# 256-column matmuls take 64 columns of each half in turn, and pages and U tiles move to other places modulo 512 bytes

## The chip, the cores and the metric

The kernel runs on one core of one Trainium2 chip. The metric is the device time of one execution in microseconds. A core has five engines that matter here: TensorE (PE in the profile; its weight loads have a row of their own, PEld), VectorE (DVE), ScalarE (ACT), GpSimd (POOL) and SyncE (SP, which issues most of the transfers). Before the change the median of three runs was 759.83 us (757.2 to 761.03).

## The reference, cut to what matters

One layer of a gated short convolution between two norms, for 1024 positions of 1024 channels, with an inner width of 2048. Everything is float32.

```python
u = rms_norm(x, pre_norm)                                  # 1024 x 1024
z, bg, cg, v = jnp.split(u @ w_in, 4, axis=-1)             # w_in 1024 x 8192
y = bg * causal_dwconv(cg * v, conv_w) * jax.nn.silu(z)    # 3 taps, 1024 x 2048
h = x + rms_norm(y @ w_out, post_norm)                     # w_out 2048 x 1024
```

So there are two large matrix products, `u @ w_in` and `y @ w_out`, and elementwise work between them.

## The kernel before, in words

**Seven products in place of eight.** Both large products are cut into blocks of two by two, and of each the kernel computes seven block products, named a to g, whose operands are sums and differences of blocks. Products a, c, d and e of `u @ w_in` always run at full block size, with 512 columns per matmul. Products b, f and g are, for most channel groups, cut a second time in the same way: seven smaller products a' to g' with 256 columns per matmul (`deep_product`, line 1463). The output product does the same: `out_mm` (line 1890) has 512 columns, and its products b and f are made of seven small ones (`small_mm`, line 1983, called by `product_b` and `product_f`).

**Three matmuls for one.** Each operand is split into a high and a low part of a reduced float32 type, and a product is the sum low*high + high*low + high*high. So each 128-row step of a product is three matmuls, each with its own weight load of 128 x 128.

**The two reads of TensorE.** In a matmul call the third argument is the moving operand (128 partitions, 256 or 512 columns of 4 bytes), the second the weights (128 partitions, 128 columns, 512 bytes in a row per partition). While one matmul streams, the weights of the next are loaded. The moving operand and the output are both rearranged by `walk` (line 865), which sets the order in which the columns are taken: `"p (h c n) -> p c h n"` with c=4 and n=4 takes 4 columns (16 bytes), jumps 64 bytes on, takes 4, and so on to the end of the row, then starts again 16 bytes further; four passes make the whole. It is the same for 256 and 512 columns.

**Where things lie.** Per partition there are seven slots of 16 KB for U tiles (`Shelves`, line 219: u_a to u_g, and later the operands of the output product, ou, oy, oA, oB, ox) and 32 pages of 2 KB (`Pages`, line 235), which hold raw weights, sums, split weights (w.., dw..) and snapshots. A pool named tmp (line 1345) holds the convolution's rows and the moving operands of the second level (`ubc` to `ugg`, tag "ub", 2 KB each, line 1412). `U_LAYOUT` (line 205) says which slots form which of two groups and how many unused bytes follow each group; `gap` (line 213) reserves them. In the built program, modulo 512 bytes: pages at 64; the slots that first hold u_b, u_f and u_g at 64; those of u_a, u_c, u_d and u_e at 384; the "ub" tiles at 448. All steps inside these tiles that a matmul addresses are multiples of 512 bytes, so a tile's place modulo 512 is that of every operand in it.

**What sets the order.** From the second channel group on, all instructions are recorded first and put in order by a planner (`Plan.arrange`), with costs and corrections in the table PLAN; every recorded call is then issued from line 292, so nearly all rows of the profile name that line, and one goes by tile names. The change does not touch the planner or its table.

**Counts.** Over 16 channel groups, b is cut again for 14, f for 13 and g for 12 (`LAST`, line 820): 39 times 7 products of 6 matmuls, 1638 matmuls of 256 columns, of which 24 of each 42 stream from a U tile (a', b', e', f') and 18 from "ub" tiles (c', d', g'). `product_b` and `product_f` add 168 each: 1974 in all, of 4320 matmuls.

Of the kernel before, what the change touches and what calls it, by code (L numbers as in the profile page):

```python
# [89 lines left out]
class View:  # L90
# [3 lines left out]
    def __init__(self, tile, steps, ids, dtype):  # L94
        self.tile, self.steps, self.ids, self.dtype = tile, steps, ids, dtype
# [104 lines left out]
class Op:  # L200
# [2 lines left out]


U_LAYOUT = (
    ((0, 3, 4), 320),
    ((1, 2, 5, 6), 192),
)
LOW_PAGES = (3, 10, 11, 13, 15, 16, 5, 6, 8, 9)
U_SLOTS = (5, 4, 2, 6, 1, 3, 0, 0, 5, 2, 6, 4, 1, 3, 0, 5, 2, 6, 4, 1, 6, 3, 0, 4, 2, 5, 6, 1, 0, 3, 2, 4, 5, 6, 0, 4, 1, 5, 3, 6, 0, 2)  # L210
# [2 lines left out]
def gap(ctx, tc, name, size):  # L213

    if size:
        ctx.enter_context(tc.tile_pool(name=name, bufs=1)).tile([128, size // 4], F32, tag=name, name=name)


class Shelves:

    def __init__(self, ctx, tc):
        self.at, self.slots = {}, list(U_SLOTS)
        for n, (slots, room) in enumerate(U_LAYOUT):
            pool = ctx.enter_context(tc.tile_pool(name=f"up{n}", bufs=1))
            self.at.update({s: pool for s in slots})
            if n == 0:
                self.low = ctx.enter_context(tc.tile_pool(name="low_pages", bufs=1))
            gap(ctx, tc, f"room{n}", room)

# [439 lines left out]
def kernel(  # L669
# [23 lines left out]
    HB = 512  # L693
# [169 lines left out]
    banks = {}  # L863

    def walk(a):
        return a.rearrange("p (h c n) -> p c h n", c=4, n=4)

    def product(p, i, ks=None):

        w = wt[p, i]  # L870
        which = {"b": "y", "e": "v", "f": "v"}.get(i, "x")
        first = i in "abe"
        if first and (p, which) not in banks:
            banks[p, which] = bank(f"p{which}_{p}")
        ps = banks[p, which]
        for k in range(KH) if ks is None else ks:
            hi, lo = (h[:, k * P : (k + 1) * P] for h in w)
            last = k == KH - 1
            nc.tensor.matmul(walk(ps), lo, walk(UH[i][:, k]), start=first and k == 0, stop=False, skip_group_check=True)
            nc.tensor.matmul(walk(ps), hi, walk(UL[i][:, k]), start=False, stop=False, skip_group_check=True)  # L880
            nc.tensor.matmul(walk(ps), hi, walk(UH[i][:, k]), start=False, stop=last, skip_group_check=True)
# [157 lines left out]

    mixed = ExitStack()  # L1040
    head = ExitStack()
    gap(ctx, tc, "room_tmp", 352)
    hp = plan.pool(head.enter_context(tc.tile_pool(name="head", bufs=1, reuse_waits="tile")), 1)

    xa = hp.tile([P, TH, D], F32, tag="xa", name="xa")
# [634 lines left out]
    for p in range(2, len(PAIRS)):  # L1680
        q, c = p + 1, p // 2
# [91 lines left out]
    for n, slot in enumerate(slots):  # L1773
        if slot[2:]:
            z, i, c = slot
# [24 lines left out]
        i, p = slot  # L1800
# [324 lines left out]
```

## Time and profile before

| | before |
|---|---|
| median of 3 runs | 759.83 us |
| the profiled execution, its own time | 758.6 us |
| its span, first to last instruction | 756.8 us |
| mean granted TensorE clock | 0.999 |
| PE busy | 744.9 us (98%), 4320 matmuls |
| PEld busy | 658.8 us (87%), 4320 loads |
| DVE busy | 677.8 us (90%) |
| ACT busy | 458.7 us (61%) |
| POOL busy | 462.4 us (61%) |

A matmul's length in the profile (some 275 ns for 256 columns, some 385 ns for 512) is longer than the distance between two of them, since they are pipelined and their ends are modelled. What a matmul costs is therefore read from the starts: the start of one run of matmuls minus the start of the run before, divided by the count. Starts are given to 0.01 us.

### The profile page before, as it was taken

The page shows a single profiled execution, that of the slowest core. Times are in us where ns is not written, and L with a number is a line of the kernel's source. Part 1 is how long each engine was busy: PE and PEld are TensorE (multiplying, and loading weights), DVE is VectorE, ACT ScalarE, POOL GpSimd, SP SyncE. Part 2 cuts the span into 40 slices and gives each one's busy share as a digit, 9 for nine tenths or more (in the row PEclk, how much of TensorE's full clock was granted, in tenths as well). Part 3 has the DMA queues.
Part 4 walks back from the last instruction along what each step waited for, and adds up shares of the span by engine and source line. Part 5 has one row for each costly group of instructions (what it writes and reads, how often), then busy time and mean ns, then how long its engine had stood idle before and what let it go on. Part 6 is the DMA issues. An engine that isn't in the chain of part 4 may idle for free.

```text
span 756.8 us, 12810 instructions
## 1 busy us (share of the span) xinstructions
PE 744.9 (98%) x4320; PEld 658.8 (87%) x4320; DVE 677.8 (90%) x1022; ACT 458.7 (61%) x880; POOL 462.4 (61%) x416
## 2 busy tenths in 40 slices
PE   8999999999999999999999999999999999999996
PEld 6888889898989899989998998999888889889885
DVE  6899998999998988989989999898999999877994
ACT  7765588675656565656556565656553656565831
POOL 2509997889685778696788677695739100600421
PEclk9999999999999999999999999999999999999999
DMA  9213325253333547576859393928465998666842
GB/s 318 74 49 91 111 75 160 103 145 125 107 119 98 174 112 209 132 192 164 258 125 269 81 256 73 272 98 223 118 179 178 343 369 307 195 227 204 281 152 111
DMA packets 117137, 130.11 MB, mean 172 GB/s; under 512 B 7320, under 2 KB 74704, under 8 KB 116944
## 3 DMA queue, kind: packets, MB, share of 16 engines
q1 hardware_dynamic: 112560, 120.77, 50.0%
q0 software_dynamic: 4352, 8.39, 7.3%
q8 instruction: 34, 0.56, 0.3%
q14 instruction: 31, 0.25, 0.1%
q10 hardware_dynamic: 160, 0.14, 0.1%
HBM read 101.74 MB, written 44.30 MB: 193 GB/s over the span
## 4 chain that ended last, share of the span: by engine, by line
PE 83%; DVE 6%; POOL 3%; issue 3%; DMA 3%; ACT 2%; SPq 0%; DVEq 0%; POOLq 0%; ACTq 0%
PE px L292 34%; PE pv L292 13%; PE po_x L292 8%; PE px2b L292 4%; PE px2f L292 3%; PE pp L292 3%; PE po_v L292 3%; PE px2g L292 3%; PE pv2b L292 2%; PE pv2f L292 2%; PE pb_x L292 1%; PE py L292 1%; PE py2b L292 1%; DMA raw<-in_sc_w_in 1%; PE pv2g L292 1%
## 5 line engine op out<-in xcount | busy, mean ns | idle before, releaser
L292 PE MATMUL px<-u_a,wah 128*128 128x512 f32 x248 | 75.8, 386 | 0.0
L292 PE MATMUL px<-u_d,wdh 128*128 128x512 f32 x248 | 75.5, 385 | 0.0
L292 PE MATMUL px<-u_c,wch 128*128 128x512 f32 x248 | 74.8, 382 | 0.0
L292 PE MATMUL pv<-u_e,weh 128*128 128x512 f32 x248 | 74.7, 381 | 0.0
L292 ACT COPY beside<-raw 128x512 f32<-128x512 f32 x67 | 39.6, 591 | 34.2 <-DVE wal L292 9.9
L292 PEld LDWEIGHTS px<-u_a,wah 128*128 128x128 f32 x248 | 46.5, 187 | 8.6
L292 PEld LDWEIGHTS px<-u_d,wdh 128*128 128x128 f32 x248 | 46.5, 187 | 8.6
L292 DVE SCALAR_TENSOR_TENSOR cv<-gpad,cw,cv 128x1024 f32<-128x1024 f32 x32 | 51.0, 1593 | 3.0 <-ACT cv L292 2.8
L292 PEld LDWEIGHTS px<-u_c,wch 128*128 128x128 f32 x248 | 46.5, 188 | 7.8
L292 PEld LDWEIGHTS pv<-u_e,weh 128*128 128x128 f32 x248 | 46.5, 188 | 7.6
L292 POOL TENSOR_TENSOR sf<-raw,sc 128x512 f32<-128x512 f32 x30 | 47.1, 1569 | 5.7 <-DVE sc L292 3.9
L292 PE MATMUL px<-u_d,wdl 128*128 128x512 f32 x124 | 48.1, 388 | 0.0
L292 PE MATMUL px<-u_a,wal 128*128 128x512 f32 x124 | 48.0, 387 | 0.0
L292 PE MATMUL px<-u_c,wcl 128*128 128x512 f32 x124 | 47.7, 384 | 0.2 <-DVE wcl L292 0.2
L292 PE MATMUL pv<-u_e,wel 128*128 128x512 f32 x124 | 47.4, 382 | 0.0
L292 POOL TENSOR_TENSOR sc<-se,raw 128x512 f32<-128x512 f32 x25 | 35.9, 1437 | 18.3 <-DVE se L292 9.4
L292 POOL TENSOR_TENSOR rs_post<-ve_post,minus_half 128x1 f32<-128x1 f32 x7 | 6.5, 941 | 65.9 <-DVE ve_post L292 65.9
L292 POOL TENSOR_TENSOR raw<-raw,raw 128x512 f32<-128x512 f32 x31 | 43.1, 1389 | 4.2 <-DVE se L292 3.8
L292 POOL TENSOR_TENSOR se<-raw,raw 128x512 f32<-128x512 f32 x22 | 31.3, 1423 | 18.1 <-DMA raw<-in_sc_w_in 13.9
L292 ACT COPY sna<-px 128x512 f32<-128x512 f32 x30 | 17.6, 585 | 35.9 <-PE px L292 32.1
L292 DVE TENSOR_TENSOR wcl<-sc,wch 128x512 fp32r<-128x512 f32 x31 | 31.9, 1028 | 5.1 <-ACT wch L292 5.1
L292 POOL TENSOR_TENSOR sne<-snc,sne 128x512 f32<-128x512 f32 x12 | 18.3, 1529 | 21.6 <-ACT snc L292 21.6
(486 smaller groups left out, 2624.5 us busy)
## 6 DMA issues: line engine op xcount, KB each, us to landing
raw<-in_sc_w_in SPq DMA_DIRECT2D x128, 256.0 KB, 5.1
y_d<-cv SPq DMA_DIRECT2D x16, 512.0 KB, 2.7
s_d<-s SPq DMA_DIRECT2D x32, 256.0 KB, 4.8
t_d<-in_sc_w_out POOLq DMA_DIRECT2D x16, 512.0 KB, 8.3
tb<-in_sc_w_out SPq DMA_DIRECT2D x16, 256.0 KB, 3.6
t_d<-in_sc_w_out SPq DMA_DIRECT2D x16, 256.0 KB, 4.8
t_d<-t_d SPq DMA_DIRECT2D x16, 256.0 KB, 4.6
s<-y_d SPq DMA_DIRECT2D x16, 256.0 KB, 4.8
```

The source lines that it names most:

```text
L292: getattr(engine, name)(*(self.plain(a) for a in args), **{k: self.plain(a) for k, a in kw.items()})
```

## The change: the column order of short matmuls, and four addresses

`walk` now tells two cases apart. For 512 columns nothing changes. For 256 columns it takes columns 0 to 63, 128 to 191, 64 to 127 and 192 to 255: runs of 64 columns (256 bytes), and between the two runs of a pair a jump to the same place of the other half, 512 bytes on. The output is walked in the same order, so the same values go to the same places.

The unused bytes are dealt out differently: a new reserve of 64 bytes ahead of the low pages, 64 and 448 bytes after the two groups of slots, and 160 in place of 352 ahead of tmp. In the built program, modulo 512 bytes, pages are then at 128, u_b, u_f and u_g (and what later lies in their slots) still at 64, u_a, u_c, u_d and u_e at 192, and the "ub" tiles at 320. Taken as the moving operand's place minus that of the weights, modulo 512:

| moving operand, weights | before | after |
|---|---|---|
| u_a, u_c, u_d, u_e; a page | 320 | 64 |
| u_b, u_f, u_g; a page | 0 | 448 (64 short of 512) |
| "ub" tiles; a page | 384 | 192 |
| output product, both in slots | 0, 192 or 320 | 0, 128 or 384 |

```diff
 U_LAYOUT = (
-    ((0, 3, 4), 320),
-    ((1, 2, 5, 6), 192),
+    ((0, 3, 4), 64),
+    ((1, 2, 5, 6), 448),
 )
...
             pool = ctx.enter_context(tc.tile_pool(name=f"up{n}", bufs=1))
             self.at.update({s: pool for s in slots})
             if n == 0:
+                gap(ctx, tc, "room_low", 64)
                 self.low = ctx.enter_context(tc.tile_pool(name="low_pages", bufs=1))
             gap(ctx, tc, f"room{n}", room)
...
     def walk(a):
-        return a.rearrange("p (h c n) -> p c h n", c=4, n=4)
+        if a.shape[-1] == HB:
+            return a.rearrange("p (h c n) -> p c h n", c=4, n=4)
+        return a.rearrange("p (h c n) -> p c h n", h=2, n=64)
...
-    gap(ctx, tc, "room_tmp", 352)
+    gap(ctx, tc, "room_tmp", 160)
```

No instruction is added, removed or moved to another place on any engine; what differs is the form of the 256-column matmuls. On PE, at the first such place of the recorded part, where product a (tile px, operand u_a, 512 columns) is followed by second-level products (px2b from a "ub" tile, pv2b from u_b), before the change:

```order
L292 MATMUL px_1176<-u_a,wal_1108 128x4x32x4
L292 MATMUL px_1176<-u_a,wah_1071 128x4x32x4 x2
L292 MATMUL px2b_1101<-ubch_deep,dwb1l_1160 128x4x16x4
L292 MATMUL px2b_1101<-ubcl_deep,dwb1h_1104 128x4x16x4
L292 MATMUL px2b_1101<-ubch_deep,dwb1h_1104 128x4x16x4
L292 MATMUL pv2b_1219<-u_b,dwb1l_1160 128x4x16x4
L292 MATMUL pv2b_1219<-u_b,dwb1h_1104 128x4x16x4 x2
```

The same rows of PE after the change (the numbers in names count tiles, and all rise by four):

```order
L293 MATMUL px_1180<-u_a,wal_1112 128x4x32x4
L293 MATMUL px_1180<-u_a,wah_1075 128x4x32x4 x2
L293 MATMUL px2b_1105<-ubch_deep,dwb1l_1164 128x2x2x64
L293 MATMUL px2b_1105<-ubcl_deep,dwb1h_1108 128x2x2x64
L293 MATMUL px2b_1105<-ubch_deep,dwb1h_1108 128x2x2x64
L293 MATMUL pv2b_1223<-u_b,dwb1l_1164 128x2x2x64
L293 MATMUL pv2b_1223<-u_b,dwb1h_1108 128x2x2x64 x2
```

Each row stands where it stood; only the 256-column forms go from 4x16x4 to 2x2x64.

## Prediction

> **What bounds the kernel now.** I read the page first: the totals of the engines, and the chain that ended last, by engine.
>
> ```profile
> span 756.8 us, 12810 instructions
> PE 744.9 (98%) x4320; PEld 658.8 (87%) x4320; DVE 677.8 (90%) x1022; ACT 458.7 (61%) x880; POOL 462.4 (61%) x416
> PE 83%; DVE 6%; POOL 3%; issue 3%; DMA 3%; ACT 2%; SPq 0%; DVEq 0%; POOLq 0%; ACTq 0%
> ```
>
> TensorE is busy for 98% of the span and is 83% of the chain. Next I asked whom it waits for (engine, tile, releaser: us in total, times, longest).
>
> ```profile
> PE pk L292 <- DVE ve_pre L292: 1.6, 1, 1.6
> PE pw L292 <- DVE idle L292: 1.1, 1, 1.1
> PE px2b L292 <- DVE dwb1l L292: 0.8, 1, 0.8
> PE pp L292 <- ACT u_a L292: 0.5, 1, 0.5
> PE pk L292 <- DVE xa L292: 0.3, 1, 0.3
> PE px L292 <- DVE u_g L292: 0.3, 1, 0.3
> PE px L292 <- DVE wcl L292: 0.2, 1, 0.2
> ```
>
> That is 4.8 us in all, most of it in the head. So the time is the sum of the distances between matmul starts, and every nanosecond by which a matmul's distance changes is paid 1974 times (256 columns) or about 2240 times (512). The change touches nothing else: instructions, order and transfers stay. So the question is what a 256-column matmul costs from start to start, and I read the start times of PE in one turn of the main part. Each row is the first of a run of twelve (start, length, tile from operands).
>
> ```profile
> 205.40 0.39 PE L292 MATMUL px<-u_c,wcl 128*128 128x512 f32 x1
> ...
> 208.04 0.27 PE L292 MATMUL px<-uggh_deep,dwg 128*128 128x256 f32 x1
> ...
> 209.42 0.38 PE L292 MATMUL pv<-u_e,wel 128*128 128x512 f32 x1
> ...
> 212.06 0.28 PE L292 MATMUL px2b<-u_b,dwb0l 128*128 128x256 f32 x1
> ...
> 213.42 0.38 PE L292 MATMUL px<-u_d,wdl 128*128 128x512 f32 x1
> ...
> 216.16 0.28 PE L292 MATMUL px2f<-u_f,dwf0l 128*128 128x256 f32 x1
> ...
> 217.53 0.39 PE L292 MATMUL px<-u_a,wal 128*128 128x512 f32 x1
> ...
> 220.27 0.28 PE L292 MATMUL px2b<-ubch_deep,dwb1l 128*128 128x256 f32 x1
> ```
>
> Differences of starts over twelve: 512 columns take 220 ns in the runs of u_c and u_e (2.64 us each) and 228 ns in those of u_d and u_a (2.74 us each), a mean of 224.2; 256 columns take 115.0 ns from "ub" tiles (1.38 us), 113.3 ns from u_b (1.36 us) and 114.2 from u_f (1.37 us). Two more stretches hold nothing but 256-column matmuls: product b of the output, whose runs of 24 the start times show, and product f, of which the table by stretches gives us, then busy and count for PE, PEld, DVE, ACT, POOL, then clock and DMA (169 is 168 and the tail of one before).
>
> ```profile
> 624.66 2.94 PE L292 MATMUL pb_x<-oB_b,oA_b 128*128 128x256 f32 x24
> 627.44 3.04 PE L292 MATMUL pb_y<-oB_b,oA_b 128*128 128x256 f32 x24
> 630.32 2.91 PE L292 MATMUL pb_x<-oB_b,oA_b 128*128 128x256 f32 x24
> 633.07 2.90 PE L292 MATMUL pb_v<-oB_b,oA_b 128*128 128x256 f32 x24
> ...
> 644.09 0.60 PE L292 MATMUL po_x<-ou_c,oy_c 128*128 128x512 f32 x2
> ```
>
> ```profile
> 687.27:706.50 19.23, 19.23 (x169) 19.23 (x168) 15.70 (x27) 12.84 (x25) 0.00 (x0) 1.00 0.70 219
> 45.00:620.00 575.00, 573.62 (x3360) 509.82 (x3359) 532.10 (x785) 353.10 (x676) 417.35 (x369) 1.00 0.57 162
> ```
>
> Product b takes 19.43 us, product f 19.23: 115.1 ns per matmul over both. Within product b the same form takes 114.6 ns (2.75 us for 24) in one run and 120 ns (2.88) in another. The clock is full and nothing is waited for, so this spread of 113 to 120 comes from how the two reads of TensorE fall together: the stream's and the weight load's, which in these stretches is busy all the time (19.23 of 19.23 us). That the load runs under the stream, one for one, is seen in single rows:
>
> ```profile
> 204.04 0.27 PE L292 MATMUL px2g<-ugch_deep,dwg1l 128*128 128x256 f32 x1
> 204.04 0.19 PEld L292 LDWEIGHTS px2g<-ugcl_deep,dwg1h 128*128 128x128 f32 x1
> 204.26 0.28 PE L292 MATMUL px2g<-ugch_deep,dwg1h 128*128 128x256 f32 x1
> 204.27 0.19 PEld L292 LDWEIGHTS px2g<-ugch_deep,dwg1l 128*128 128x128 f32 x1
> ```
>
> The load of the next weights starts in the same hundredth of a microsecond as the matmul that it runs under, or one later.
>
> **The change part by part. The 256-column matmuls.** Today's bill: 936 that stream from a U tile (39 x 24) at 113.3 ns are 106.0 us, 702 from "ub" tiles (39 x 18) at 115.0 are 80.7, and 336 in the output product at 115.1 are 38.7: 225.4 us. No row shows the new order, so I bound it. From below: the best sustained rate of the trace is 220 ns for 512 columns, so 110 for 256, which makes 217.1 us, a gain of 8.3. The Trainium skill ("TensorE: Matmul & The Clock Gate", Back-to-back issue gap) gives N/2.4 + 2.5 ns at full clock, which is 109.2 ns, and by it the most to gain would be 9.9 us; the same formula gives 215.8 for 512 columns, which no sustained run here reaches. From above: the worst sustained row is 120 ns, which makes 236.9 us, a loss of 11.5.
>
> To choose between the ends I follow the two reads through one matmul of about 110 ns, an estimate from the addresses of the diff. Modulo 512 bytes the load sweeps the 512 bytes once, at 4.65 bytes per ns; the stream reads 1024 bytes, at 9.3. In the old order the stream crosses all 512 bytes every 32 columns, eight times per matmul, so it passes the load's place seven or eight times whatever the distance, which agrees with distances of 0 and 384 both lying at 113 to 115. In the new order it stays within 256 bytes for the first half of the matmul (twice through), and within the other 256 for the second, as the load does with its own halves. From "ub" tiles (distance 192) the stream's place is 192 + 9.3t, then from 192 again at a quarter of the time, then from 448: the load is passed in no quarter. So I let these lose nearly all their excess and take 110.5 ns, a gain of 702 x 4.5 = 3.2 us. From U tiles (448, that is 64 bytes behind the load) the stream passes the load in the first quarter unless it leads by 64/9.3 = 7 ns. The rows above let the lead be anything from nothing to some 15 ns. I take it that it leads, and 110.5 ns too: 936 x 2.8 = 2.6 us. In the output product (0, 128, 384) places coincide only where runs begin or end; I take 112, a gain of 336 x 3.1 = 1.0 us. Sum: 6.8 us, between a gain of 8.3 and a loss of 11.5.
>
> **The 512-column matmuls.** Their order stays, their distance goes from 320 to 64 (1488 of them: a, c, d, e, 31 runs of 12 each) or from 0 to 448. That distance matters to them is seen in the output product, whose runs of 96 stand in the chain of waits (start, length):
>
> ```profile
> 644.25 21.73 PE po_x L292 x96
> 665.98 21.45 PE po_v L292 x96
> ```
>
> By the slots, all of the first run has distance 0 and takes 226.4 ns per matmul; half of the second has 0 and half 320, which leaves 220.5 for 320. But u_c and u_a, both at 320, differ by 8 ns too, so what went before counts as much. No row has distance 64. I take no change, with ends of all 1488 at 220 (a gain of 1488 x 4.2 = 6.2 us) and all at 228 (a loss of 5.7).
>
> **What is late next.** From 45 to 620 us DVE is busy for 532.10 of 575.00 us and PE without work for 1.4. A PE that is 1% faster leaves DVE at 93 to 94%; I let 0.5 us come back as waits. If that cover were gone, the whole gain would be lost, not more. Other engines read and write at new places too; their distances to one another hardly change, and a stall there of up to the planner's few us of lead is hidden under PE: nothing.
>
> **Sum.** The profiled execution took 758.6 us, its span 756.8 and 1.8 around it. 758.6 - 6.8 + 0.5 = 752.3. It lies 1.2 under the median of the runs, so the median should come to 753.5.
>
> **The rivals.** *The stream runs up behind the load (slower).* If the stream from U tiles has no lead, it starts 64 bytes behind, meets the load after 14 ns and has 128 bytes of its run left; if the load goes first, these pass at the load's pace, 27.5 ns in place of 13.8. By the third quarter it is 128 bytes behind and meets the load only at the run's end. So 13.8 ns more, 936 times: 12.9 us, less 3.2 from "ub" tiles: 759.8 + 9.7 = 769.5. It decides at a lead of 7 ns. For it: loads that start in the very same hundredth. Against: where the row of the load is the later one. *The two reads don't meet at all (no change).* The Trainium skill (the same page, Step-by-step: what each phase is for) says that TensorE has two independent read ports and that loading the next weights takes no read bandwidth from the running matmul. A mechanism in which neither order nor place counts gives 759.8. Against it stand equal forms at full clock that differ: 220 and 228, 114.6 and 120. *The 512-column matmuls take it back.* With all 1488 at 228 ns, 6.3 - 5.7 = 0.6 us are left: 759.2. For it: half the runs shown stand at 228 already.
>
> **How the numbers follow.** A measurement of this kernel can tell about 0.5%, 3.8 us. The forecast has 0.55, its own range from 747.5 (the whole 8.3, and two thirds of the 512-column end) to 757; the slower rival 0.22, from 763 to 785; the independent reads 0.12; the 512 columns 0.11. Below 756.0 lies all but 0.02 of the forecast, and 0.01 of the last rival: faster 0.54. Within 0.5% lie the two rivals of no change, but for that 0.01, and 0.02 of the forecast: 0.24. Slower: 0.22. The range from 747 to 767 leaves out some 0.03 below and, of the slower rival, some 0.14 above.
>
> **What would show it.** In the profile after, the runs of twelve from "ub" tiles should take 1.33 us from start to start, and those from u_b and u_f as well; the stretches of products b and f 18.8 us each; the runs of u_c and u_e 2.64 as now. Runs of u_b of 1.48 us or more would show the slower rival; runs that keep their 1.36 and 1.38 the independent reads; runs of 2.74 throughout, with short runs faster, the third. Matmul waits of several us on DVE or ACT would show that the cover is gone. The forecast is wrong if the U-tile runs don't get shorter, or if any wait of PE above 2 us is new.

## The result and the profile after

| | before | after |
|---|---|---|
| median of 13 runs each | 759.19 us (757.2 to 761.03) | 762.32 us (760.51 to 763.65) |
| ratio after to before | | 1.004, 95% interval 1.0029 to 1.0052 |
| profiled execution, its own time | 758.6 us | 763.1 us |
| its span | 756.8 us | 761.3 us |

The change makes the kernel 0.4% slower: 3.1 us by the medians, 4.5 us between the two profiled executions. The forecast was 753.5 us, 6.3 us under the 759.83 known then. One later execution (of e2) ran at a granted clock of 0.85 and took 838 us; it is left out of the times below. The page of after shows TensorE as full as before, with 3.4 us more of busy time:

```profile
PE 748.3 (98%) x4320; PEld 661.0 (87%) x4320; DVE 676.6 (89%) x1022; ACT 459.0 (60%) x880; POOL 462.8 (61%) x416
```

The same turn of the main part that the prediction read, in the timeline of after (start, length, tile from operands; each row is the first of a run of twelve):

```profile
205.27 0.38 PE L293 MATMUL px<-u_c,wcl 128*128 128x512 f32 x1
...
207.95 0.28 PE L293 MATMUL px<-uggh_deep,dwg 128*128 128x256 f32 x1
...
209.32 0.38 PE L293 MATMUL pv<-u_e,wel 128*128 128x512 f32 x1
...
212.00 0.28 PE L293 MATMUL px2b<-u_b,dwb0l 128*128 128x256 f32 x1
...
213.38 0.38 PE L293 MATMUL px<-u_d,wdl 128*128 128x512 f32 x1
...
216.05 0.28 PE L293 MATMUL px2f<-u_f,dwf0l 128*128 128x256 f32 x1
...
217.43 0.38 PE L293 MATMUL px<-u_a,wal 128*128 128x512 f32 x1
...
220.11 0.28 PE L293 MATMUL px2b<-ubch_deep,dwb1l 128*128 128x256 f32 x1
```

The 256-column runs take 1.37 us ("ub" tiles), 1.38 (u_b) and 1.38 (u_f), where 1.38, 1.36 and 1.37 stood: nothing gained, nothing lost. The 512-column runs, which were 2.64 or 2.74 us, are now all 2.67 or 2.68: u_d and u_a won what u_c and u_e lost.

So where do 4.5 us come from? Four matmuls serve as landmarks, the same in both kernels: the first of the run of u_d at 123 us, of u_a at 397, of u_c at 550 and the first of the output product at 603. Before, then after:

```profile
123.38 0.50 PE L292 MATMUL px<-u_d,wdl 128*128 128x512 f32 x1
...
396.66 0.39 PE L292 MATMUL px<-u_a,wal 128*128 128x512 f32 x1
...
549.79 0.46 PE L292 MATMUL px<-u_c,wcl 128*128 128x512 f32 x1 [0.21 <-DVE wcl L292]
...
603.22 2.17 PE L292 MATMUL po_x<-ou_a,oy_a 128*128 128x512 f32 x9
```

```profile
123.28 0.47 PE L293 MATMUL px<-u_d,wdl 128*128 128x512 f32 x1
...
396.56 0.38 PE L293 MATMUL px<-u_a,wal 128*128 128x512 f32 x1
...
551.55 0.46 PE L293 MATMUL px<-u_c,wcl 128*128 128x512 f32 x1 [0.17 <-DVE wcl L293]
...
605.04 0.38 PE L293 MATMUL po_x<-ou_a,oy_a 128*128 128x512 f32 x1
```

| stretch, us | before | after | |
|---|---|---|---|
| start to the first landmark | 123.38 | 123.28 | -0.1 |
| main part, from u_d at 123 to u_a at 397 | 273.28 | 273.28 | 0.0 |
| on to u_c at 550 | 153.13 | 154.99 | +1.9 |
| on to the output product | 53.43 | 53.49 | +0.1 |
| output product to the end | 153.57 | 156.24 | +2.7 |

The output product's part is in the rows of TensorE itself. In the start times of after, products b and f lie between these rows, and behind them stand the long runs of products c and e:

```profile
626.95 3.04 PE L293 MATMUL pb_x<-oB_b,oA_b 128*128 128x256 f32 x24
...
647.00 21.80 PE L293 MATMUL po_x<-ou_c,oy_c 128*128 128x512 f32 x96
668.64 22.10 PE L293 MATMUL po_v<-ou_e,oy_e 128*128 128x512 f32 x96
690.58 3.01 PE L293 MATMUL pf_x<-oB_f,oA_f 128*128 128x256 f32 x24
...
710.60 21.88 PE L293 MATMUL po_x<-ou_d,oy_d 128*128 128x512 f32 x96
```

Product b takes 20.05 us (19.43 before), product f 20.02 (19.23): 119.3 ns per matmul in place of 115.1, 1.4 us more in both. The 512-column run of c keeps its time (21.64; 21.73 before), that of e goes from 21.45 to 21.94. The other 512-column runs of the product lose 0.9 us more (a: from 21.44 to 21.91; d and g together 0.4).

The end of the main part lost its 1.9 us to waits. TensorE's waits of after between 395 and 600 us (engine, tile, releaser: us in all, times, longest) come to 2.5 us with a last one of 0.2. Before has 1.3 there: the rows of px2b, of px behind u_g and of px behind wcl that the prediction shows.

```profile
PE px L293 <- DVE u_g L293: 1.0, 1, 1.0
PE px2b L293 <- DVE dwb1l L293: 0.7, 1, 0.7
PE px L293 <- ACT beside L293: 0.3, 1, 0.3
PE px L293 <- DVE wcl L293: 0.3, 2, 0.2
```

Taken from the start times (what is over the usual distance), the waits between the 2800th and the 3230th matmul are 1.0 us before and 2.9 us after.

### The profile page after: what moved, and what is told of

Same layout as the page of the kernel before. It is cut to its first block, busy times and chain, and to the rows that moved or that the text cites. A ratio compares the mean times of both kernels' runs of the same rounds, so it can differ in the third digit from the quotient of the medians.

```text
span 761.3 us, 12811 instructions
## 1 busy us (share of the span) xinstructions
PE 748.3 (98%) x4320; PEld 661.0 (87%) x4320; DVE 676.6 (89%) x1022; ACT 459.0 (60%) x880; POOL 462.8 (61%) x416
## 4 chain that ended last, share of the span: by engine, by line
PE 89%; DVE 3%; DMA 2%; POOL 2%; ACT 2%; issue 1%; SPq 0%; POOLq 0%; ACTq 0%; DVEq 0%
PE px L293 35%; PE pv L293 14%; PE po_x L293 11%; PE px2b L293 4%; PE px2f L293 3%; PE po_v L293 3%; PE px2g L293 3%; PE pp L293 3%; PE pv2f L293 2%; PE pv2b L293 2%; PE pf_x L293 2%; PE pb_x L293 2%; DMA raw<-in_sc_w_in 1%; PE py2b L293 1%; PE py L293 1%
## 5 line engine op out<-in xcount | busy, mean ns | idle before, releaser
L293 POOL TENSOR_TENSOR sf<-raw,sc 128x512 f32<-128x512 f32 x30 | 45.0, 1499 | 7.5 <-DVE sc L293 5.7
L293 POOL TENSOR_TENSOR sc<-se,raw 128x512 f32<-128x512 f32 x25 | 35.9, 1434 | 18.3 <-DVE se L293 9.4
L293 POOL TENSOR_TENSOR cv<-cv,sne 128x512 f32<-128x512 f32 x13 | 17.7, 1364 | 23.1 <-DVE cv L293 21.9
```

The costliest lines, as they stand in the source:

```text
L293: getattr(engine, name)(*(self.plain(a) for a in args), **{k: self.plain(a) for k, a in kw.items()})
```

## The experiments

The theories at the outset. *Place*: in the new order a matmul's cost hangs on the distance between the moving operand and the weights, and the distances of the output product are bad ones. *Order*: the new order costs the same wherever the operands lie. *Layout*: the 512-column matmuls, which only moved, do it all. "Distance" is used of places (moving operand minus weights, in bytes) and of starts (in ns). A matmul form is "settled" when its start distances repeat in a pattern, which is called a cycle here; a settled value is the mean of the last 24 start distances of a run.

**e1_walk_alone and e2_layout_alone: each half of the change by itself.**

```diff
 # e1: before, and
-        return a.rearrange("p (h c n) -> p c h n", c=4, n=4)
+        if a.shape[-1] == HB:
+            return a.rearrange("p (h c n) -> p c h n", c=4, n=4)
+        return a.rearrange("p (h c n) -> p c h n", h=2, n=64)
 # e2: after, and the same lines taken out again
```

> The addresses of before with the new order of the 256-column matmuls. My theory now, from the profile of after: in the new order what counts is the distance of moving operand and weights modulo 128 bytes; at an odd multiple of 64 (after: U tiles 448, second-level tiles 192) a matmul settles at 113.3 ns, at an even one (after: output product 0, 128, 384) at some 119.5. In the addresses of before all second-level products lie at an even multiple (0 and 384), so 1638 matmuls go from 114.4 to 119.5, some 8 us more, and product f (0 and 192) and b (0 and 320) are halfway, some 0.5 us more each: about 768 us. Rival, the new order costs the same whatever the place: then 759.2 plus what it does in after, at most 762. Rival, the layout does it all by the 512-column matmuls: 759.2, as before.

> The addresses of after with the old order throughout. My theory: the 512-column matmuls are those of after (runs of u_a and u_d shorter, of u_c and u_e longer, the output product 1.6 us longer), together some 1.2 us over before; the 256-column matmuls in the old order stay near 114.5 whatever the distance: 760.4 us. Rival, the layout does it all: 762.3, as after. Rival, the order does it all: 759.2, as before.

The order alone: 764.59 us, ratio 1.0067 (1.0047 to 1.0087). The addresses alone: 760.09 us, ratio 1.0011 (0.9995 to 1.0026). In the timeline of e1, a run of twelve of u_b and the run behind it:

```profile
213.55 0.28 PE L292 MATMUL px2b<-u_b,dwb0l 128*128 128x256 f32 x1
...
214.98 0.39 PE L292 MATMUL px<-u_d,wdl 128*128 128x512 f32 x1
```

The run of u_b takes 1.43 us, 119 ns per matmul; over the kernel the second-level matmuls average 118.4 ("ub") to 118.9 (u_g), where after has 114.1 to 114.9 with the same order. So the same order costs different amounts at different places: *Order* is out. All 256-column matmuls together take 7.8 us more in its profile, about as forecast; TensorE's waits are 1.2 shorter, and the span is 6.6 longer. The median is only 5.4 us over before, where some 9 were expected. The addresses alone are not told apart from before: the interval, up to 761.2 us, leaves out the 762.3 of *Layout* and holds the 760.4 of *Place* as well as no change at all.

**e3_table: matmuls alone, by order and distance.** A kernel of its own; its core:

```python
lhs = w[:, (512 if part == 0 else 0) + step * 128 :][:, :k]        # weights, k columns
at = (ROOM // 4 if part == 1 else 0) + step * 512 + d // 4          # moving, d bytes further on
nc.tensor.matmul(walk(ps[:k, :cols], w_out), lhs, walk(m[:, at : at + cols], w_in), ...)
```

> A kernel of matmuls alone, 55 runs of 39 after 60 for warming up, none of the reference's work, its output not the reference's: each run has one order of columns for the moving operand and the output, one distance of moving operand minus weights modulo 512 (0 to 448 in steps of 64), 256 or 512 columns, with steps and pairs of tiles as in the kernel. My theory: 256 columns in the new order take 113.3 ns per matmul at 64, 192, 320 and 448 and 119.5 to 120 at 0, 128, 256 and 384; in the old order 113 to 116 everywhere. Rival, the place doesn't count and the spread in the kernel comes from what goes before: then all runs of one form take the same to 1 ns. With weights of 64 columns in place of 128 the distances between starts fall towards 110 ns if the weight load takes part, and stay if the moving operand's own order sets them.

In its timeline a name gives columns, order of the operand and of the output (o old, n new), columns of weights (k) and distance (d). Start differences over 39 (38 at distance 0):

```profile
27.67 4.71 PE L69 MATMUL m256nnk128d0x<-m,w 128*128 128x256 f32 x38
32.22 8.77 PE L69 MATMUL m512ook128d0x<-m,w 128*128 128x512 f32 x38
...
54.00 4.75 PE L69 MATMUL m256nnk128d64x<-m,w 128*128 128x256 f32 x39
58.59 8.74 PE L69 MATMUL m512ook128d64x<-m,w 128*128 128x512 f32 x39
...
80.58 4.79 PE L69 MATMUL m256nnk128d128x<-m,w 128*128 128x256 f32 x39
85.21 9.10 PE L69 MATMUL m512ook128d128x<-m,w 128*128 128x512 f32 x39
...
107.66 4.59 PE L69 MATMUL m256nnk128d192x<-m,w 128*128 128x256 f32 x39
112.09 9.00 PE L69 MATMUL m512ook128d192x<-m,w 128*128 128x512 f32 x39
...
324.38 4.58 PE L69 MATMUL m256nnk64d0x<-m,w 128*64 128x256 f32 x39
328.81 4.58 PE L69 MATMUL m256ook64d0x<-m,w 128*64 128x256 f32 x39
```

Settled distances in ns, all of that kind; 256, 320, 384 and 448 give the same as 0, 64, 128 and 192 to 0.1 ns, but for the old order at 0 and 256 (0.6 and 0.8, since 24 starts don't hold whole cycles there):

| | 0 | 64 | 128 | 192 |
|---|---|---|---|---|
| 256 columns, old order | 116.4 | 117.2 | 114.6 | 114.5 |
| 256 columns, new order | 120.0 | 117.8 | 118.6 | 113.3 |
| 512 columns, old order | 227.1 | 220.0 | 230.0 | 227.0 |
| 512 columns, order of the new form | 226.7 | 228.9 | 232.3 | 233.3 |

*Place* holds, but not in the form that I gave it: 64 is not as good as 192; what counts is the distance modulo 256. After's 448 and 192 are both 192 there, the best of the new order; its output product lies at 0 and 128, the worst. The order of the output counts too: with the operand contiguous and the output in the new order, or the other way round, 256 columns take 113.3 ns at 448, but with both contiguous 117.8 at 192; at 0 and 64 all of these take the same. With half the weight columns the new order at distance 0 falls from 120.0 to 113.3 ns, the old from 116.4 to 113.3: the excess goes with the load (at 64, though, the new order keeps 116.7 of 117.8). But no run lies below 113.3 or 220.0. Between these two least values 256 columns more cost 106.7 ns; taken off 113.3, that leaves 6.67 ns per matmul that do not grow with the columns (worked out from these two lengths; no third was run).

**e5_output_old_order: after, with the old order in the output's small products.**

```diff
 # small_mm only
-                nc.tensor.matmul(walk(ps), lo, walk(uh[:, k]), ...)
+                nc.tensor.matmul(walk_old(ps), lo, walk_old(uh[:, k]), ...)
```

> After, with the old order in products b and f of the output alone (336 matmuls of 256 columns); the new order stays in the 1638 second-level ones. By the table of matmuls alone, the new order takes 120.0, 118.6 ns at 0 and 128 modulo 256 and 113.3 at 192; the output product lies at 0 and 128, the rest at 192. My theory: 336 matmuls go from 119.3 back to some 115, 1.4 us less: 760.9 us, still above before by what the 512-column matmuls lose. Rival, the second-level matmuls lose as well and the output product has only its share: 762.0.

Products b and f fall to 19.42 us (626.22 to 645.64) and 19.38, as before the change: 1.3 us, nearly the 1.4 expected. The long runs of e and g, whose form stays, get 0.2 and 0.4 us shorter as well (21.94 to 21.76, 21.84 to 21.41), so that part of what the long runs lost hung on the short ones ahead of them. The median shows little of it: 762.03 us, ratio 1.0037 (1.0023 to 1.0051); that overlaps after's 1.0029 to 1.0052. What the products take is shown; that the time falls with it is not.

**e6_table_finer: other orders, and places between.**

> Matmuls alone as in the first table, 82 runs of 27: distances between the steps of 64 bytes, and other orders of the columns (2, 4 or 8 columns at a time, in passes of other lengths) at 0, 64, 128 and 192. Its output is not the reference's. Theory: what is gained or lost comes in steps of 8 cycles of 1.2 GHz (6.67 ns) per matmul or per few matmuls, 113.3 and 220 ns being the least at one step over 106.7 and 213.3; then no run settles below these. Rival: another order or a place between the steps of 64 goes below 113.3 or 220.

Nothing settled below 113.3 or 220.0. Places between the steps of 64 give means of 220.9 to 230.6 ns for 512 columns in the old order; at 144 and 208 the last distances stand at 220. One order reaches both least values at one place, distance 0: 8 columns (32 bytes), then 128 bytes on ("a" in the names; 27 matmuls a run):

```profile
139.09 6.11 PE L67 MATMUL m512aak128d0x<-m,w 128*128 128x512 f32 x27
145.03 3.22 PE L67 MATMUL m256aak128d0x<-m,w 128*128 128x256 f32 x27
148.09 6.36 PE L67 MATMUL m512aak128d64x<-m,w 128*128 128x512 f32 x27
```

5.94 us over 27 are 220.0 ns, 3.06 over 27 are 113.3. (Orders of 2 columns, 8 bytes, at a time take 430 ns and more for 512 columns.)

**e7_replay: one turn of TensorE's order without any other work.**

> One turn of the main part (222 matmuls of one group's order on TensorE, 96 of 512 columns and 126 of 256) played 32 times without any other work, the 512-column operands always at 64 from the weights (modulo 512), U tiles b, f, g at 0, 64, 128 or 192, second-level tiles at 0, 64, 128 or 192, the 256 columns in the old or the new order. Its output is not the reference's. Theory: TensorE's own reads set the distances and nothing that other engines do; then the turns with the addresses of before (0 and 128, old), of after (192 and 192, new), of the order alone (0 and 128, new) and of the addresses alone (192 and 192, old) show per form what the kernels show: 512 columns at 223, 223, 223.5 and 222.3 ns, 256 columns at 114.4, 114.6, 118.6 and 114.4. Rival, the other engines' reads and writes take part: then the turns are shorter, and all alike to 0.5%.

The name gives the order (o, n) and the places of 512-column operands, U tiles b, f, g and second-level tiles. The first rows of the turns of e2 and e1, each with the turn behind it:

```profile
561.79 2.84 PE L83 MATMUL oa64b192d192x<-ua,w 128*128 128x512 f32 x12
597.46 2.80 PE L83 MATMUL na64b0d0x<-ua,w 128*128 128x512 f32 x12
...
670.20 2.84 PE L83 MATMUL na64b0d128x<-ua,w 128*128 128x512 f32 x12
706.56 2.84 PE L83 MATMUL na64b0d192x<-ua,w 128*128 128x512 f32 x12
```

The replayed turn takes 35.67 us with the addresses alone and 36.36 with the order alone. In the kernels the same turn, from one run of u_a to the next but one, takes 35.64 (e2) and 36.36 (e1); before has 35.83 and after 35.83, the replays of their turns 35.9 and 35.8. The replay has next to no work of DVE, ACT and POOL and no transfers beside its turns, so TensorE's distances in the main part come from TensorE's own work to some 0.2%.

**e8_eight_at_one_place and e9_short_eight: a version drawn from the table, and its small half.**

```diff
 # e8: before, and
 U_LAYOUT = (
-    ((0, 3, 4), 320),
-    ((1, 2, 5, 6), 192),
+    ((0, 3, 4), 0),
+    ((1, 2, 5, 6), 0),
 )
...
-        return a.rearrange("p (h c n) -> p c h n", c=4, n=4)
+        return a.rearrange("p (h c n) -> p c h n", c=4, n=8)
...
-    gap(ctx, tc, "room_tmp", 352)
+    gap(ctx, tc, "room_tmp", 480)
 # e9: before, and
-        return a.rearrange("p (h c n) -> p c h n", c=4, n=4)
+        return a.rearrange("p (h c n) -> p c h n", c=4, n=8 if a.shape[-1] < HB else 4)
```

> A version drawn from the finer table: in both sizes the order takes 8 columns (32 bytes), jumps 128 bytes on, and so on in four passes, and pages, all U slots and second-level tiles lie at the same place modulo 512 (all distances 0, the output product's as well). Matmuls alone settle at 220.0 and 113.33 ns there, both the least of any run. Theory, TensorE's reads set the time: 1974 x (114.5 - 113.3) = 2.4 us and 2243 x (223.8 - 220.1) = 8.3 us less, 10.7 in all, of which the other engines, DVE above all, give back 2 to 4 as waits: 751 to 753 us. Rival, cover: what TensorE gains comes back as waits one for one, 757 or more. Rival, in the kernel the switches between the two sizes keep the long runs from 220: 755 and more.

> Before, with only the 256-column order changed to 8 columns at a time with jumps of 128 bytes; addresses as before, so U tiles b, f, g at 0, second-level tiles at 128 and the output product at 0, 64 and 192 (modulo 256), where matmuls alone take 113.3, 113.4, 115.0 and 119.0 ns. The second-level matmuls lose 1638 x 1.0 = 1.7 us, the output product gains or loses up to 0.7, the 512-column matmuls are entered in another state and may land at 220 or at 228: between 754 and 762 us, which the replay of a turn in this order (64, 0, 128, short 8 and long 4) is to tell beforehand by its 512-column distance.

> The turn of 222 matmuls again, 38 times: short matmuls in the order of 8 columns, long ones in it too with their operand at 0, or in the old order with theirs at 64, U tiles b, f, g and second-level tiles at 0, 64, 128 and 192; and six mixed turns. Output not the reference's. Theory: with all at 0 and 8 columns throughout, 512-column matmuls stay at 220 to 220.5 and 256-column ones at 113.3, a turn of 96 x 220.3 + 126 x 113.4 = 35.4 us against 36.0 with the addresses and order of before. Rival: the switches hold the long runs in another cycle, and the turn takes 35.7 or more.

e8 took 773.22 us, ratio 1.0178 (1.0164 to 1.0193): slower by more than anything else here. In its turn:

```profile
214.17 0.39 PE L292 MATMUL pv<-u_e,wel 128*128 128x512 f32 x1
...
216.93 0.28 PE L292 MATMUL px2b<-u_b,dwb0l 128*128 128x256 f32 x1
```

The run of u_e takes 2.76 us, 230 ns per matmul, at the order and place that took 220.0 alone. The replay has the same (512 columns at 229.6 ns, its turn 36.7 us; the kernel's 36.73). Single distances show it: alone, a long run at 220 repeats 219 and 221; the output product's runs of 96 in e8 repeat 230, 230, 237, 227, 229 (230.6 on the mean) and never leave that. So the same form at the same place has more than one cycle in which it can stay. What the turn has beside the table's runs are the switches between the two lengths, which agrees with the rival; e15 below tests it.

e9 took 759.30 us, ratio 0.9996 (0.9981 to 1.0011). Its landmarks:

```profile
123.01 0.44 PE L292 MATMUL px<-u_d,wdl 128*128 128x512 f32 x1
...
394.65 0.38 PE L292 MATMUL px<-u_a,wal 128*128 128x512 f32 x1
...
549.53 0.46 PE L292 MATMUL px<-u_c,wcl 128*128 128x512 f32 x1 [0.21 <-DVE wcl L292]
```

The main part takes 271.64 us, 1.6 less than before (here the long runs are left at 220.4 ns on the mean in place of 223.1; the replay had 220.3), and the stretch behind it 154.88, 1.8 more: the lead is gone in waits. The output part is 0.6 us longer, since this order is a poor one at its distance of 192.

**e11_before_again and e12_after_again: a second profile of each.**

> Before once more, for a second profile. Between matmul 2800 and 3230 (some 491 to 563 us) TensorE's waits over the usual distances come to 1.0 us in the profile of before, 2.4 with the short order of 8 columns, and 2.2 to 3.0 in the three kernels with the addresses of after. Theory, these waits belong to the addresses or the pace of a kernel: 1.0 again within 0.4. Rival, they differ from run to run: a value of 2 or more.

> After once more, for a second profile. Theory, the waits of 2.9 us between matmul 2800 and 3230 belong to the kernel: 2.5 to 3.3 again, and the matmul distances by place are those of the first profile to 0.2 ns. Rival, they differ from run to run: 1.5 or less.

TensorE's own distances repeat: main part 273.86 (0.5 of it a wait) and 273.47 us, products b and f 19.36 and 19.31 against 20.05 and 20.02. The waits between matmul 2800 and 3230 were 1.5 and 3.6 us (1.0 and 2.9 in the first profiles). In these profiles they belong to the kernels, with some 0.6 us of play. Of before's output product, the long runs of c and e do not repeat as well: 226.3 and 223.4 ns in the first profile, 224.8 and 225.1 in the second.

**e13_same_distances_moved and e14_after_moved: the place of tiles as such.**

```diff
 # both
+    gap(ctx, tc, "room_first", 64)
     shelves = Shelves(ctx, tc)
 # e13 only: before, and
-    ((0, 3, 4), 320),
-    ((1, 2, 5, 6), 192),
+    ((0, 3, 4), 64),
+    ((1, 2, 5, 6), 448),
...
-    gap(ctx, tc, "room_tmp", 352)
+    gap(ctx, tc, "room_tmp", 96)
```

> Before's order of columns, with the addresses moved so that every distance of moving operand and weights stays the same modulo 256 (0, 64 and 128) while pages lie at 128 and u_a, u_c, u_d, u_e at 192 modulo 512, as in after. Theory, TensorE's distances depend on the difference modulo 256 alone: each form within 0.2 ns of before, products b and f 19.4 and 19.2 us. Of the waits between matmul 2800 and 3230 (1.0 and 1.5 us in the two profiles of before, 2.9 and 3.6 in those of after): if the place of pages and tiles as such makes the other engines later, 2.2 or more, and the time 761 us; if not, 1.0 to 1.6, and 759.5 us.

> After with all tiles 64 bytes further on (pages at 192, u_a, u_c, u_d, u_e at 256, the second-level tiles at 384 modulo 512), so that every distance between tiles stays. TensorE's distances stay those of after to 0.2 ns. If the waits of 2.9 to 3.6 us hang on the place of pages at 128 as such, they fall below 2 and the time to 761; if they hang on distances (of whatever engine) or on the pace of TensorE, they stay at 2.5 to 3.6 and the time at 762.3.

e13: 759.29 us, ratio 0.9992 (0.9978 to 1.0006), every form of the main part within 0.4 ns of before, products b and f 19.36 and 19.30 us (all long runs of the output but g's as in before's second profile), waits 1.3 us. e14: 762.28 us, ratio 1.0031 (1.0013 to 1.0049), products b and f 20.05 and 20.02 as in after. So TensorE's distances follow the difference of addresses modulo 256, not the places themselves, and pages at 128 as such do not make the other engines late. But e14's waits were 1.6 us in that stretch and 3.5 between the first landmark and it, where after has 2.0: their place moves within the kernel. All waits behind the first landmark come to 3.6, 4.1 and 3.6 us in before, e11 and e13, and to 5.0, 6.5 and 5.1 in after, e12 and e14.

**e15_entry_scan: can the cycle be chosen?**

```python
first = 0 if name in ("c1", "d1") else v                  # v = 0 to 11
form = "o" if n < first else "e"                          # n-th matmul of a long run at distance 0
```

> The output product's matmuls alone (products a to f and d in the kernel's order, with before's distances), 13 times: once in the old order throughout, then with 256 columns in the order that the tables show least for each place (8 columns at 0, 64 of each half at 192, old at 64), and the 512-column runs at distance 0 in the order of 8 columns after their first 0 to 11 matmuls in the old one. Its output is not the reference's. Theory: the state in which a run is entered decides between the cycles of 220 and of 230 ns, and the count of matmuls ahead changes it, so some counts give runs near 220 and others near 230. Rival, the form and the place decide: all counts give the same, 220 or 230. In the old order the 512-column matmuls at 0 stay at 226 to 227, and those at 64 at 220 to 224.

It can, when the stage is played alone. Start differences over 48; names give v and the product. With v = 0, product a's first run takes 220.0 ns per matmul and c's 230.6; with v = 5, c's takes 221.0:

```profile
155.15 10.73 PE L51 MATMUL v0a0x<-ua,w 128*128 128x512 f32 x48
165.71 10.89 PE L51 MATMUL v0a1x<-ua,w 128*128 128x512 f32 x48
...
195.71 11.23 PE L51 MATMUL v0c0x<-ua,w 128*128 128x512 f32 x48
206.78 11.23 PE L51 MATMUL v0c1x<-ua,w 128*128 128x512 f32 x48
...
823.27 10.76 PE L51 MATMUL v5c0x<-ua,w 128*128 128x512 f32 x48
833.88 10.72 PE L51 MATMUL v5c1x<-ua,w 128*128 128x512 f32 x48
```

Over all 13 settings the stage took 123.4 us (v = 5) to 126.5 (v = 1), 125.1 in the old order.

**e16_output_steered and e17_both: the versions that this points to.**

```diff
 # both: before, and in out_mm
+            w0, w1, w2 = (eight if (i, h) in AT_ZERO and (q or 3 * k + j >= AT_ZERO[i, h]) else walk for j in range(3))
 # AT_ZERO: 5 for a, c, d, 2 for e, 0 for the second halves of c and d
 # small_mm: eight at distance 0, halves_walk (64 of each half) at 192, old at 64
 # e17 only
-        return a.rearrange("p (h c n) -> p c h n", c=4, n=4)
+        return a.rearrange("p (h c n) -> p c h n", c=4, n=8 if a.shape[-1] < HB else 4)
```

> Before's addresses and main part; only the output product's order of columns is chosen by place: 256 columns as in the scan, 512 columns at distance 0 in the order of 8 columns after 5 (a, c, d) or 2 (second half of e) matmuls in the old one. No wait of TensorE lies in this part, so that its gain should be paid out. In the scan this part took 123.4 us in place of 125.5. Theory, the entry state is the same as in the scan: runs at 220 to 221 ns, the stage 2.1 to 2.6 us shorter, 757.2 us against 759.5. Rival, the waits ahead of it in the kernel leave another state and runs fall into the cycle of 230: no gain or a loss of up to 1 us.

> The same output part, and in the main part the second-level matmuls in the order of 8 columns as in e9, which brought TensorE 2.2 us ahead by 408 us and lost it again to waits by 560. Theory, the main part's gain is given back to the other engines again: the time of the steered output alone, within 0.7 us. Rival, some of it stays: a further 1 to 2 us less.

e16: 759.87 us, ratio 1.0004 (0.9991 to 1.0017). Its output part, 146.06 us from the first output matmul to the last, is only 0.4 shorter than before's 146.45. The first half of c came to 221.1 ns as in the scan, but its second half to 231.8 and a's first half to 229.2, where the scan had 220.0 and 220.6: the state on entry was not the scan's. e17: 757.63 us, ratio 0.9967 (0.9952 to 0.9982), faster than before by 2.1 us in the same rounds, and 2.2 us under e16, where 0.7 at most was expected. Its landmarks:

```profile
123.73 0.51 PE L292 MATMUL px<-u_d,wdl 128*128 128x512 f32 x1 [0.24 <-DVE wdl L292]
...
396.43 0.38 PE L292 MATMUL px<-u_a,wal 128*128 128x512 f32 x1
...
549.53 0.47 PE L292 MATMUL px<-u_c,wcl 128*128 128x512 f32 x1 [0.19 <-DVE wcl L292]
```

Main part 272.70, the stretch behind it 153.10: 0.6 us of the main part's gain stays here and 0.5 us comes from the output part. Its profiled execution shows 0.8 us less span than before's, its median 2.1 less time; e9 and e16 together would promise some 0.1 us at their medians. How much of the 2.1 is the waits' play from run to run is not settled.

## Why the prediction was wrong, point by point

- **What bounds the kernel** was right: the time is the sum of TensorE's distances plus few waits, and the replay shows for the main part that the distances come from TensorE alone.
- **The floor is the step that failed.** "The best sustained rate of the trace is 220 ns for 512 columns, so 110 for 256" halved a distance of which a part does not halve: the least values are 220.0 and 113.3 ns in every table, so that 6.67 ns stay per matmul. The bill was also drawn up from single runs (113.3 for U tiles, 115.0 for "ub" tiles); over the kernel all 256-column matmuls stood at 114.5 ns. They had 1.2 ns each, 2.3 us in all, to give up, not 8.3; in the second-level ones, at 114.4 on the mean, 1.7. The Trainium skill ("TensorE: Matmul & The Clock Gate", Back-to-back issue gap) puts the gap of an isolated matmul at 2.5 ns over N/2.4. No form settled here below 113.3 ns for 256 columns, where that formula gives 109.2.
- **The passes of the two reads.** That the place counts and that the load takes part was right: the new order settles at the floor at 192 and at 118 to 120 elsewhere, and at distance 0 a load of half the width takes the excess away. That passes are what costs is not shown, and the rule failed at 0 and 128, where it saw little to lose and the new order is worst; the output's order, which it left out, counts as well. The places count modulo 256, not 512, so that U tiles "64 bytes behind the load" are simply at 192, like the second-level tiles. A gain of 5.8 us was forecast for both; after the change they take 114.1 to 114.9 ns, much as before it, since at each switch from a 512-column run two matmuls take 118 to 124 ns before the run settles at 113.3.
- **The output product's short matmuls** were mis-sized, with the wrong sign: "places coincide only where runs begin or end; I take 112" met 119.3, 1.4 us more in place of 1.0 less. Its distances of 0 and 128 are the two worst of the new order. This is shown by the table, by e5 and by e1, where part of it lay at 192 (19.7 and 19.8 us).
- **The 512-column matmuls** "no change" held in the main part to 0.1 us, as a sum: 320 and 64 are the same place modulo 256, and what shifted is in which cycle each run is left (u_a and u_d 1.8 to 2.6 ns less, u_c and u_e 2.2 to 2.7 more). In the output product they lost 1.3 us between the two profiles, which the sum left out.
- **What is late next** was put at 0.5 us; 1.9 us came, though TensorE had won nothing up to there. e9 shows the same stretch taking a real lead of 1.6 us. In that stretch DVE is busy for 94% of the time in before, so little is needed. What makes the other engines later in after is open. Second profiles repeat it, and e13 speaks against the tiles' places as such. The profile of e2 has the same 2.9 us of waits there with the addresses alone, that of e1 1.1 with the order alone (but its TensorE comes there some 4 to 5 us later); so they seem to come with the new addresses, whether by the distances of other engines' tiles or by TensorE's local pace.
- **The rivals.** The stream that runs up behind the load (769.5) did not come: at 448 the runs of u_b took 1.38 us. Losses of some 4 ns, not of its 13.8, came at other places, 0 and 128, in e1 (118.4 to 118.9 ns). The independent reads gave the nearest time (759.8) for a wrong reason: by the Trainium skill (the same page, Step-by-step: what each phase is for) a load takes no read bandwidth from the running matmul, and here the same matmuls took 113.3 to 120.0 ns by place alone, and 113.3 again with a load of half the width. The third, 512 columns taking it back, is not what happened in the main part.

By the sum: forecast -6.8 and +0.5; in the two profiles 0.0 in the main part, +2.7 in the output product, +1.9 in waits, -0.1 elsewhere. So of the 11 us or so between the 752.3 of the sum and the 763.1 of the profiled execution, 5.8 are the gain in the second-level matmuls that did not come, 2.4 the output's short matmuls, 1.3 its long ones and 1.4 the waits.

## What to carry to other kernels

A kernel that is bound by back-to-back matmuls can be measured piece by piece: a table of matmuls alone by order and place, and a replay of TensorE's order alone, gave the main part's turn of each of the six kernels that it played to 0.3%. The replay of the output stage (e15) did not carry over as well. A least value of such a table is no forecast for a kernel that switches forms: e8 had the best cell for both lengths and was 1.8% slower. And a gain of the engine that bounds a stage may not be paid out where another is nearly as busy: e9 lost in waits behind DVE and the others what it had won, e17 kept 0.6 us of it.

## What the runs showed of the hardware that was not expected

- Moving operand and weights act on one another by the difference of their addresses modulo 256 bytes: e3 in eight distances, e13 in the kernel (each form of the main part within 0.4 ns of before).
- Many settled means stand 6.67 ns or half of it apart (113.3, 116.7, 120.0 for 256 columns; 220.0, 226.7, 230.0, 233.3 for 512), but 114.5, 118.6 and 228.9 occur as well, so that no fixed step is shown.
- One form at one place can stay in different cycles (220.0 or 230.6 ns for 512 columns, 8 at a time, distance 0), chosen by the matmuls ahead of it.
- The number of columns taken at a time can double the cost: at distance 0, 256 columns take 113.3 ns 8 at a time and 217.8 ns 2 at a time (e6; operand and output in the same order).
